# Hybrid diffusion backbone: the last products of the chunk inverse placed between two halves of a recurrence step, and two PSUM users moved to another pool

## The chip, the cores and the metric

One core of one Trainium2 chip runs the whole program. Its engines each work through a queue of their own, in a fixed order: PE (TensorE, matrix products), DVE (VectorE), ACT (ScalarE), POOL (GpSimd), and SP, which here issues the DMAs. The metric is the device time of one execution in microseconds. The kernel before takes 4563.76 us (median of 3 runs, 4554.51 to 4570.26).

## The reference, cut to what matters

Two layers. In each a token mixer and a channel mixer; the change is in the token mixer, which runs two groups of heads side by side over 1024 latent tokens and 256 context tokens: attention (8 heads), and RWKV-7, a linear recurrence in both directions (8 heads of 64). In float32:

```
def step(s, inp):                                   # one token
    r_t, w_t, k_t, v_t, kk_t, a_t = inp
    sa = einsum('bhvk,bhk->bhv', s, kk_t)
    s = (s * w_t[:, :, None, :]
         - sa[..., None] * (kk_t * a_t)[:, :, None, :]
         + v_t[..., None] * k_t[:, :, None, :])
    return s, einsum('bhvk,bhk->bhv', s, r_t)       # state, output
...
for d in range(2):                                  # both directions
    s_ctx, y_c = wkv_scan(..context.., s0, rev=d)
    _, y_l = wkv_scan(..latent.., s_ctx, rev=d)
m_lat = concat([rwkv_output(y_lat[0] + y_lat[1], ..), mla_lat]) @ w_o
```

The two outputs per token (one per direction) are added, normalised per head, gated, put beside the attention's output, and go through one output projection.

## The kernel before, in words

Each layer runs as stages: input projection, mixer, output projection, channel mixer. Only the mixer is touched. It mixes two kinds of work that need nothing of each other.

Attention is cut into pairs of heads `h` and tiles of 128 queries `t`: 40 pieces in layer 0, 32 in layer 1. A piece (`attn`, lines 1037 to 1124) makes scores `sp` on PE (L1075), takes their extreme on DVE (`mx`, L1076), the exponential on ACT (`P`, L1088), transposes it on PE (`tp`, L1107), copies that on DVE or ACT (`pT`, L1112 and L1110), multiplies it with the values on PE (`av`, L1117), and ends with `o` on DVE (L1123).

The recurrence is cut into chunks of 64 tokens: ten steps `i` of 128 tokens, each of two halves `c`, both directions and all heads at once. A step has four parts.

- Preparation, `rwkv_prep`: loads `KR`, `BK`, `W` from DRAM, makes the chunk's products `g` (L884) and transposes `bt` (L894) on PE, masks them on DVE (`KR`, `GA`, L887 and L890) and copies the rest on ACT (`AB`, `BT`).
- Inverse, `rwkv_inv`: `Dg` on ACT (L911), the transpose `Dt` on DVE (L913), then 31 dependent pairs of DVE operations on `T` (L925, L926), and the transposes `TD` (L928) and `X` (L932).
- Last products of the inverse, `rwkv_inv2`: `p1` (L945) needs `TD`; its result goes through ACT and DVE into `AB`; `p2` (L953) needs that; its result goes into `X`. Only the sequence of the same step uses that `X`.
- Sequence, `rwkv_seq(i, c)`: Z (L977, copied at L979), X times Z (L984, to `W` at L985 and L986), the new state (L991, `St` L996, `W` of the next half L999, `S` L1001). Beside that chain the outputs `y` (L1009 and L1014, evicted to `ysb` at L1021 or L1024). L1009 is the last reader of a step's `KR`.

`rwkv_out` normalises and gates `ysb` of the later visits to a block and writes it to DRAM (L838); the output projection (L1187, L1228) reads that.

Two things set the order of the work. The mixer's code order: two preparations ahead, then for each step its share of attention, `rwkv_seq(i, 0)`, `rwkv_seq(i, 1)`, `rwkv_inv2(i + 1)`, `rwkv_prep(i + 2)`. From that the layer underneath fixes an order per engine when the program is built: it takes what is ready in its own reckoning, earlier code first, and waits where a buffer is still held. Buffers of one tag are handed out in code order. PSUM is 8 banks: `Rp` has two for tag "r" (`g`, `bt`, the `ro` of `rwkv_out`), `Rq` one for tag "q" (every product of `rwkv_seq`, and `p1`, `p2`), attention has five. `KR` has two buffers for each direction, so step `i + 2` loads into what step `i` held; `BK` and `AB` have two, `Dg`, `Dt`, `T`, `TD` one.

Of the kernel before, what the change touches and what calls it, by code (L numbers as in the profile page):

```python
# [7 lines left out]
F32 = mybir.dt.float32  # L8
# [14 lines left out]
NP = 4  # L23
# [50 lines left out]
def bc(ap, shape):  # L74
    return ap.to_broadcast(shape)
# [6 lines left out]
class Kern:  # L82
# [675 lines left out]
    def mixer(self, l, wst):  # L758
        tc = self.tc
        with ExitStack() as st:  # L760
            R = self.R = Ctx()
            R.pp = st.enter_context(tc.tile_pool(name=f"Rp{l}", bufs=2, space=PSUM, reuse_waits="tile"))
            R.pq = st.enter_context(tc.tile_pool(name=f"Rq{l}", bufs=1, space=PSUM, reuse_waits="tile"))
            self.attn_setup(l, st)
            self.rwkv_setup(l, st)
            need_ctx = l < DEPTH - 1
            order = ([8, 9] if need_ctx else []) + [3, 4, 2, 5, 1, 6, 0, 7]
            work = [(h, t) for h in range(NP) for t in order]
            done = 0
            self.rwkv_prep(l, 0)  # L770
            self.rwkv_inv2(l, 0)
            self.rwkv_prep(l, 1)
            for i in range(10):

                upto = len(work) * (i + 1) // 10 if i < 9 else len(work)
                for h, t in work[done:upto]:
                    self.attn(l, h, t, t == order[0])
                done = upto
                self.rwkv_seq(l, i, 0)
                self.rwkv_seq(l, i, 1)  # L780
                if i < 9:
                    self.rwkv_inv2(l, i + 1)
                if i == 8:
                    R.sr.close()
                    self.load_wo(l, wst)
                if i < 8:
                    self.rwkv_prep(l, i + 2)
                for o in R.out:
                    self.rwkv_out(*o)
                R.out = []  # L790
# [144 lines left out]
    def rwkv_inv2(self, l, i):  # L935

        nc = self.nc
        R = self.R
        pp, cst = R.pp, self.cst
        AB, TD = R.inv  # L940
        X = R.X[i % 2]
        ps = R.pq.tile([128, 16, 32], F32, name="p1", tag="q")
        for u in range(16):
            for q0 in (0, 64):
                nc.tensor.matmul(ps[q0 + 32:q0 + 64, u, :], AB[q0:q0 + 32, u, 32:64], TD[q0:q0 + 32, u, :],  # L945
                                 start=True, stop=True)
        nc.scalar.activation(AB[96:128, :, 0:32], ps[96:128], AF.Copy, scale=-1.0)
        nc.vector.tensor_scalar(AB[32:64, :, 0:32], ps[32:64], -1.0, None, op0=ALU.mult)
        ps = R.pq.tile([128, 16, 32], F32, name="p2", tag="q")
        for u in range(16):  # L950
            for q0 in (0, 64):
                r = slice(q0 + 32, q0 + 64)
                nc.tensor.matmul(ps[q0:q0 + 32, u, :], AB[r, u, 0:32], X[r, u, 32:64], start=True, stop=True)  # L953
        nc.scalar.activation(X[0:32, :, 32:64], ps[0:32], AF.Copy)
        nc.vector.tensor_copy(X[64:96, :, 32:64], ps[64:96])

    def rwkv_seq(self, l, i, c):

        nc = self.nc
        R = self.R  # L960
        p, pp = R.p, R.pq
        X = R.X[i % 2]
        half = [slice(0, 64), slice(64, 128)]
        tgs = self.groups(i)
        out_y = l < DEPTH - 1 or tgs[0] < 8
        KR, GA, W, BT, PC = R.st.pop((i, c))
        nxt = R.st.get((i + c, 1 - c))
        S = R.S
        dq = [(d, q) for d in range(2) for q in range(NP)]
        psum = lambda: pp.tile([128, 2, NP, 64], F32, name="q", tag="q")  # L970
        if S is None:
            for e in range(2):
                nc.vector.memset(W[half[e], e], 0.0)
        ps = psum()
        for d, q in dq:
            for e in range(2):
                nc.tensor.matmul(ps[half[e], d, q, :], KR[d][:, e, q, c, :], W[:, e, d, q, :], start=True, stop=True)  # L977
        Z = p.tile([128, 2, NP, 64], F32, name="Z", tag="Z")
        nc.vector.tensor_copy(Z, ps)  # L979
        ps = psum()  # L980
        for d, q in dq:
            for e in range(2):
                he = half[e]
                nc.tensor.matmul(ps[he, d, q, :], X[he, (d * 2 + c) * 4 + q, :], Z[he, d, q, :], start=True, stop=True)  # L984
        nc.scalar.activation(W[half[0], 0], ps[half[0]], AF.Copy, scale=-1.0)  # L985
        nc.vector.tensor_scalar(W[half[1], 1], ps[half[1]], -1.0, None, op0=ALU.mult)  # L986
        if nxt is not None:
            ps = psum()
            for d, q in dq:
                for e in range(2):  # L990
                    nc.tensor.matmul(ps[half[e], d, q, :], BT[d][:, q, e, :], W[:, e, d, q, :], start=True, stop=True)  # L991
            St = p.tile([128, 2, NP, 64], F32, name="St", tag="Z")
            if S is None:
                nc.vector.tensor_copy(St, ps)
            else:
                nc.vector.tensor_tensor(St, ps, S, op=ALU.add)  # L996
            pb = bc(PC[:, :, :, None], [128, 2, NP, 64])
            for e, eng in ((0, nc.vector), (1, nc.gpsimd)):
                eng.tensor_tensor(nxt[2][half[e], e], St[half[e]], pb[half[e]], op=ALU.mult)  # L999
            R.S = p.tile([128, 2, NP, 64], F32, name="S", tag="S", bufs=2)  # L1000
            nc.gpsimd.tensor_tensor(R.S, St, pb, op=ALU.mult)  # L1001
        if out_y:
            py = psum()

            if S is not None:
                for d, q in dq:
                    for e in range(2):
                        he = half[e]
                        nc.tensor.matmul(py[he, d, q, :], S[he, d, q, :], KR[d][he, 2, q, c, :], start=(d, q) == dq[0],  # L1009
                                         stop=False, skip_group_check=True)  # L1010
            for d, q in dq:
                for e in range(2):
                    he = half[e]
                    nc.tensor.matmul(py[he, d, q, :], W[:, e, d, q, :], GA[d][:, e, q, :],  # L1014
                                     start=S is None and (d, q) == dq[0], stop=(d, q) == dq[-1], skip_group_check=True)
            ysb = p.tile([128, 2, NP, 64], F32, name="ysb", tag="ysb", bufs=2)
            if self.second(l, i):
                y0 = p.tile([128, 2, NP, 64], F32, name="y0", tag="y0")
                for d, tg in enumerate(tgs):
                    nc.sync.dma_start(out=y0[:, d], in_=self.yD[l][2 * tg + (1 - c if d else c)])  # L1020
                nc.vector.tensor_tensor(ysb, py, y0, op=ALU.add)  # L1021
                R.out.append((l, i, c, ysb))
                return
            nc.scalar.activation(ysb, py, AF.Copy)  # L1024
            for d, tg in enumerate(tgs):
                nc.sync.dma_start(out=self.yD[l][2 * tg + (1 - c if d else c)], in_=ysb[:, d])
# [441 lines left out]
```

## Time and profile before

| | |
|---|---|
| median of 3 runs | 4563.76 us |
| the profiled execution's own time | 4568.71 us |
| its span, first to last instruction | 4566.9 us |
| mixer of layer 0 | about 690 to 1411 us of the span |
| mixer of layer 1 | about 3007 to 3700 us |

The busy time of an engine is the time in which at least one of its instructions ran. The stretches of the two mixers are taken from the first attention work to the last result of the recurrence (L835), and the output projection's first product (L1228) stands after them. A wait is named by what ended it; where a step's result waits for another engine, the row of the waiting instruction names that engine and line.

### The profile page before, as it was taken

Reading aid. Unit: us, or ns where it says so; the run is one execution under the profiler, and the core shown is the slowest. Engines: PE = TensorE matmul, PEld = TensorE weight load, DVE = VectorE, ACT = ScalarE, POOL = GpSimd, SP = SyncE. Lnnn points to the kernel's source line nnn. Section 1 sums busy time; section 2 is a strip of 40 time slices with the busy share of each in tenths; the row PEclk is TensorE's granted clock in tenths of the full one; section 3 lists DMA queues with packets and bytes.
Section 4 is the critical chain, followed back from the end, with each engine's and each line's share of the span. In section 5 each row is a group of like instructions: output and inputs, shape, how many; then the busy total and the mean of one; then the engine's idle time right before and its main releaser. Section 6 shows DMA issues by size and latency. Waiting matters only on the chain. (4 is left out here: it accounts for less than half of the span.)

```text
span 4566.9 us, 72983 instructions
## 1 busy us (share of the span) xinstructions
PE 4159.5 (91%) x29598; PEld 3294.7 (72%) x29598; DVE 2736.5 (60%) x4943; ACT 1688.5 (37%) x3000; POOL 541.9 (12%) x492
## 2 busy tenths in 40 slices
PE   8978888888888899999998989988889878999998
PEld 5756656676766788888886866666777666888887
DVE  3225567888885534554447235569887866555456
ACT  3213455444554432221224224454445534222222
POOL 1000000111222300000004000001111244000002
PEclk9998889899998999999998998989998989999999
DMA  6652234323324211111113222343232243111111
GB/s 222 237 180 91 104 120 125 84 69 81 79 61 140 100 37 35 40 42 33 47 35 111 84 71 100 117 144 77 61 81 66 65 136 126 54 51 51 44 50 65
DMA packets 425698, 401.36 MB, mean 88 GB/s; under 512 B 243473, under 2 KB 329937, under 8 KB 425361
## 3 DMA queue, kind: packets, MB, share of 16 engines
q1 hardware_dynamic: 425360, 396.69, 28.1%
q8 instruction: 233, 3.82, 0.3%
q14 instruction: 105, 0.85, 0.1%
HBM read 285.85 MB, written 110.72 MB: 87 GB/s over the span
## 5 line engine op out<-in xcount | busy, mean ns | idle before, releaser
L1279 PE MATMUL up<-u,hi 128*128 128x512 f32 (+1 forms) x3520 | 1012.6, 369 | 4.2 <-ACT hi L1269 4.2
L1279 PEld LDWEIGHTS up<-u,hi 128*128 128x128 f32 x3520 | 643.8, 189 | 119.8 <-ACT hi L1269 4.6
L1279 PE MATMUL up<-u,lo 128*128 128x512 f32 (+1 forms) x1760 | 648.5, 368 | 0.0
L304 PE MATMUL pj<-u,whi 128*128 128x512 f32 (+1 forms) x1888 | 567.2, 385 | 36.0 <-DVE o L325 31.0
L1326 DVE TENSOR_TENSOR acc<-dn,acc 128x512 f32<-128x512 f32 x340 | 233.3, 688 | 432.9 <-PE dn L1320 432.8
L304 PEld LDWEIGHTS pj<-u,whi 128*128 128x128 f32 x1888 | 352.6, 198 | 139.4 <-issue 45.2
L1279 PEld LDWEIGHTS up<-u,lo 128*128 128x128 f32 x1760 | 332.1, 189 | 57.9 <-DVE lo L1271 0.3
L304 PE MATMUL pj<-u,wlo 128*128 128x512 f32 (+1 forms) x944 | 360.0, 382 | 0.1
L1075 PE MATMUL sp<-ka,qa 96*128 96x512 f32 (+1 forms) x1200 | 320.8, 399 | 37.2 <-ACT P L1088 26.1
L1269 ACT ACTIVATE hi<-raw 128x512 fp32r<-128x512 f32 x176 | 110.5, 630 | 564.4 <-PE up L1279 561.4
L1320 PE MATMUL dn<-hi,fh 128*128 128x512 f32 x792 | 311.8, 394 | 7.9 <-ACT fh L1294 4.0
L1320 PE MATMUL dn<-lo,fh 128*128 128x512 f32 x792 | 310.0, 391 | 0.0
L1320 PE MATMUL dn<-hi,fl 128*128 128x512 f32 x792 | 305.9, 390 | 0.0
L1088 ACT ACTIVATE P<-sp,mx 128x512 f32<-128x512 f32 (+1 forms) x400 | 240.0, 607 | 174.1 <-DVE mx L1085 98.4
L1117 PE MATMUL av<-pT,va 128*64 128x128 f32 x2624 | 235.5, 302 | 51.3 <-DVE pT L1112 25.5
L1075 PEld LDWEIGHTS sp<-ka,qa 96*128 96x128 f32 x1200 | 214.8, 205 | 89.6 <-ACT P L1088 38.5
L1107 PE MATMUL tp<-cst,P 128*128 128x128 f32 x1312 | 236.7, 303 | 22.5 <-ACT P L1088 16.4
L1076 DVE TENSOR_REDUCE mx<-sp 128x1 f32<-128x512 f32 (+1 forms) x400 | 229.4, 586 | 39.7 <-PE sp L1075 37.1
L1117 PEld LDWEIGHTS av<-pT,va 128*64 128x64 f32 x2624 | 152.0, 146 | 108.6 <-DVE pT L1112 31.7
L1271 DVE TENSOR_TENSOR lo<-raw,hi 128x512 fp32r<-128x512 f32 x176 | 125.4, 715 | 173.8 <-ACT hi L1269 161.3
L287 ACT ACTIVATE whi<-raw 128x512 fp32r<-128x512 f32 (+2 forms) x110 | 66.1, 602 | 435.7 <-PE pj L304 384.5
L304 PEld LDWEIGHTS pj<-u,wlo 128*128 128x128 f32 x944 | 186.6, 198 | 39.2 <-issue 7.3
(254 smaller groups left out, 7233.5 us busy)
## 6 DMA issues: line engine op xcount, KB each, us to landing
wt<-in_w_ada_dram SPq DMA_DIRECT2D x96, 512.0 KB
raw<-in_w_up_dram SPq DMA_DIRECT2D x176, 256.0 KB
raw<-in_w_down_dram SPq DMA_DIRECT2D x88, 256.0 KB
raw<-in_w_in_dram SPq DMA_DIRECT2D x84, 256.0 KB
bkD<-lt SPq DMA_DIRECT2D x32, 640.0 KB
BK<-bkD SPq DMA_DIRECT2D x320, 64.0 KB
KR<-kkD SPq DMA_DIRECT2D x152, 128.0 KB
kkD<-kx SPq DMA_DIRECT2D x16, 640.0 KB
```

The lines of the kernel that those rows point to most:

```text
L287: nc.scalar.activation(hi[:, :m], raw[:, :m], AF.Copy)
L304: nc.tensor.matmul(ps[:, o:o + n], ww, u[k][s], start=k == 0 and j == 0, stop=k == nk - 1 and j == 2)
L1075: nc.tensor.matmul(sp[:, o - b0:o - b0 + n], q[:, qq, e], A.k[e][:, kk, o:o + n], start=m == 0, stop=m == 2)
L1076: nc.vector.tensor_reduce(mx[:, i:i + 1], sp[:, :w], axis=AX.X, op=ALU.min)
L1088: nc.scalar.activation(P[:, o:o + w], sp[:, :w], AF.Exp, bias=mn, scale=-1.0, accum_out=mx[:, 4 + i:5 + i])
L1107: nc.tensor.transpose(tp[:, b, e], Ps[e][:, o:o + 128], self.ident)
L1117: nc.tensor.matmul(av[half[e], 0:128], A.v[:, k0 // 128 + kt, half[e]], pT[:, b, e], start=kt == 0, stop=kt == nkt - 1)
L1269: nc.scalar.activation(hi, raw, AF.Copy)
L1271: nc.vector.tensor_tensor(lo, raw, hi, op=ALU.subtract)
L1279: nc.tensor.matmul(ps[:, so:so + sn], ww, uu[k][s], start=k == 0 and m == 0, stop=k == 7 and m == 2)
L1320: nc.tensor.matmul(ps, x[:, t * 128:(t + 1) * 128], w, start=m == 0, stop=m == 3 * len(js) - 1)
L1326: nc.vector.tensor_tensor(dst, ps, dst, op=ALU.add)
```

## The change

Three edits. `rwkv_inv2(i + 1)` now stands between the two halves of step `i` in the code. Its `p1` and `p2` take banks of tag "r" in place of tag "q". The outputs `y` of `rwkv_seq` do so too. No instruction is added or taken away, and no size changes.

```
                 self.rwkv_seq(l, i, 0)
-                self.rwkv_seq(l, i, 1)
                 if i < 9:
                     self.rwkv_inv2(l, i + 1)
+                self.rwkv_seq(l, i, 1)
...
-        ps = R.pq.tile([128, 16, 32], F32, name="p1", tag="q")
+        ps = pp.tile([128, 16, 32], F32, name="p1", tag="r")
...
-        ps = R.pq.tile([128, 16, 32], F32, name="p2", tag="q")
+        ps = pp.tile([128, 16, 32], F32, name="p2", tag="r")
...
         if out_y:
-            py = psum()
+            py = R.pp.tile([128, 2, NP, 64], F32, name="y", tag="r")
```

The order on PE in layer 0 around the outputs of step 7's second half (L1009 and L1014 into `q`), before; `g` in the last row but two is the first of step 9's preparation:

```order
L991 MATMUL q<-W,BT 64x64 x16
L1117 MATMUL av<-pT,va 64x128 x4
L1107 MATMUL tp<-cst,P 128x128 x4
L1075 MATMUL sp<-ka,qa 128x512 x6
L1075 MATMUL sp<-ka,qa 128x256 x3
L1009 MATMUL q<-KR,S 64x64 x16
L1014 MATMUL q<-GA,W 64x64 x16
L1117 MATMUL av<-pT,va 64x128 x4
L1107 MATMUL tp<-cst,P 128x128 x4
L884 MATMUL g<-KR,BK 128x128 x8
L1075 MATMUL sp<-ka,qa 128x512 x3
L1117 MATMUL av<-pT,va 64x128 x4
```

`p1` of step 8 stands 13 rows after that first `g`. The same outputs in the changed kernel (L1009 and L1014 now into `y`), with `p1` and `p2` of step 8 (L945, L953):

```order
L1107 MATMUL tp<-cst,P 128x128 x4
L945 MATMUL p_11935<-TD,AB 32x32 x32
L1117 MATMUL av<-pT,va 64x128 x4
L1120 MATMUL av<-cst,mx 64x128 x2
L1107 MATMUL tp<-cst,P 128x128 x4
L953 MATMUL p_11970<-X_4537,AB 32x32 x32
L1009 MATMUL y<-KR,S 64x64 x16
L1014 MATMUL y<-GA,W 64x64 x16
L984 MATMUL q<-Z,X_4537 64x64 x9
L884 MATMUL g<-KR,BK 128x128 x4
```

The outputs of a step's second half have moved behind `p1` and `p2` of the next step, and the `g` of the step after that stands behind them. It is so at all 16 such places of the two layers that have outputs; at the two in layer 1 that have none (its context steps), `g` stands behind `p2` too.

The order on DVE in layer 0 at the start of step 9's inverse (the last one), before:

```order
L979 COPY Z<-q 128x512
L1076 TENSOR_REDUCE mx<-sp 128x1
L1112 COPY pT<-tp 128x512
L913 STREAM_TRANSPOSE Dt<-Dg 128x1024
L1123 TENSOR_TENSOR o_12607<-av,o_12607 128x128
L1076 TENSOR_REDUCE mx<-sp 128x1
L925 TENSOR_TENSOR tmp<-Dt,T 128x31
L1085 TENSOR_REDUCE mx<-mx 128x1
L926 TENSOR_TENSOR T<-T,tmp 128x31
```

and in the changed kernel:

```order
L986 TENSOR_SCALAR W<-q 64x512
L913 STREAM_TRANSPOSE Dt<-Dg 128x1024
L996 TENSOR_TENSOR St<-q,S 128x512
L925 TENSOR_TENSOR tmp<-Dt,T 128x31
L833 TENSOR_TENSOR ysb<-ysb,sq 128x512
L999 TENSOR_TENSOR W<-St,pc_91 64x512
L926 TENSOR_TENSOR T<-T,tmp 128x31
L1123 TENSOR_TENSOR o_13677<-av,o_13677 128x128
L925 TENSOR_TENSOR tmp<-Dt,T 128x30
```

Before, 180 of layer 0's 208 score reductions (L1076) stand ahead of this `Dt`; in the changed kernel all 208 do, and the `o` in the fence is the last of the 40 pieces of attention. In layer 1 the same holds one step sooner: ahead of `Dt` of step 8 stood 148 of 192 reductions, and now stand all 192. On every engine the output projection begins behind the last instruction of the mixer, in both orders.

## Rows read from the trace of the kernel before

**Rows 1.** The page's head: span and instructions.
```profile
span 4566.9 us, 72983 instructions
```
**Rows 2.** Busy time by stretch: us, then each engine's busy us, PEclk, DMA share, GB/s.
```profile
690.00:1411.00 721.00, 627.74 (x8076) 492.86 (x8074) 582.52 (x1526) 375.05 (x870) 123.57 (x139) 0.93 0.33 84
1080.00:1120.00 40.00, 38.47 (x560) 31.26 (x561) 34.82 (x91) 22.84 (x58) 5.02 (x7) 1.00 0.27 68
1381.00:1411.00 30.00, 21.61 (x244) 15.53 (x240) 13.17 (x23) 17.59 (x30) 7.30 (x6) 0.76 0.36 99
3007.00:3700.00 693.00, 604.29 (x7674) 476.61 (x7673) 560.24 (x1465) 349.89 (x808) 111.50 (x126) 0.91 0.31 81
```
**Rows 3.** PE in order of time, one round: start, us, line, operation; wait in brackets.
```profile
1128.39 1.15 PE L1009 MATMUL q<-KR,S 64*64 64x64 f32 x32
1129.47 1.15 PE L1014 MATMUL q<-GA,W 128*64 128x64 f32 x32
1131.21 0.66 PE L1107 MATMUL tp<-cst,P 128*128 128x128 f32 x4
1133.32 1.99 PE L884 MATMUL g<-KR,BK 64*128 64x128 f32 x16 [1.45 <-DMA KR<-kkD]
...
1175.20 1.15 PE L977 MATMUL q<-W,KR 128*64 128x64 f32 x32 [0.37 <-DVE ysb L1021]
...
1205.28 1.20 PE L945 MATMUL p<-TD,AB 32*32 32x32 f32 x64 [0.28 <-DVE TD L928]
1209.22 1.20 PE L953 MATMUL p<-X,AB 32*32 32x32 f32 x64
```
**Rows 4.** DVE in order of time, the same round.
```profile
1161.88 1.98 DVE L913 STREAM_TRANSPOSE Dt<-Dg 128x1024 f32<-128x1024 f32 x1 [0.43 <-ACT Dg L911]
1168.26 0.68 DVE L999 TENSOR_TENSOR W<-St,pc 64x512 f32<-64x512 f32 x1
...
1204.15 1.07 DVE L928 STREAM_TRANSPOSE TD<-T 128x512 f32<-128x512 f32 x1
```
**Rows 5.** PE in order of time: `p1` of steps 0 and 9, both layers.
```profile
789.27 1.20 PE L945 MATMUL p<-TD,AB 32*32 32x32 f32 x64 [2.04 <-DVE TD L928]
1350.22 1.92 PE L945 MATMUL p<-TD,AB 32*32 32x32 f32 x64
3101.57 1.20 PE L945 MATMUL p<-TD,AB 32*32 32x32 f32 x64
3642.69 1.92 PE L945 MATMUL p<-TD,AB 32*32 32x32 f32 x64
```
**Rows 6.** Groups on DVE, layer 0's mixer: busy us, mean ns of one, idle before.
```profile
L926 DVE TENSOR_TENSOR T<-T,tmp 128x126 f32<-128x126 f32 (+22 forms) x310 | 100.4, 324 | 5.7
L925 DVE TENSOR_TENSOR tmp<-Dt,T 128x126 f32<-128x126 f32 (+22 forms) x310 | 92.4, 298 | 5.2
L887 DVE TENSOR_TENSOR KR<-g,cst 64x256 f32<-64x256 f32 x80 | 33.5, 419 | 21.3 <-PE g L884 20.5
L890 DVE TENSOR_TENSOR GA<-g,cst 128x256 f32<-128x256 f32 x80 | 33.2, 415 | 0.6
```
**Rows 7.** In order of time: the ends of both mixers, and ACT's split of `w_o`.
```profile
1361.01 1.14 ACT L755 ACTIVATE hi<-raw 128x512 fp32r<-128x512 f32 x2
1391.97 1.97 PE L1009 MATMUL q<-KR,S 64*64 64x64 f32 x32 [2.31 <-DVE W L986]
1397.32 1.14 ACT L755 ACTIVATE hi<-raw 128x512 fp32r<-128x512 f32 x2
1408.59 1.26 POOL L835 TENSOR_TENSOR ysb<-ysb,gt 128x512 f32<-128x512 f32 x1 [3.37 <-DMA gt<-gD]
1411.39 0.29 DVE L1123 TENSOR_TENSOR o<-av,o 128x128 f32<-128x128 f32 x1 [4.87 <-ACT o L1122]
1418.74 3.78 PE L1228 MATMUL ps<-hi,mh 128*128 128x512 f32 x8 [7.71 <-ACT mh L1187]
3699.46 1.26 POOL L835 TENSOR_TENSOR ysb<-ysb,gt 128x512 f32<-128x512 f32 x1 [3.66 <-DMA gt<-gD]
```

## The prediction

> **What bounds the kernel now.** I read the page first (its span [rows 1]; the profiled execution took 4568.7 us, 1.8 more than the span and 5 more than the median of the runs), then busy time by stretch, then the two mixers in order of time, engine by engine, and last the groups of DVE. Only the mixers matter, since nothing outside them is edited. In both the reader is to see that two engines are full nearly all the time: in layer 0 PE is busy 627.74 of 721 us (87%) and DVE 582.52 (81%), in layer 1 604.29 and 560.24 of 693 [rows 2]. Attention fills whatever the recurrence leaves. Both end together: the last `o` of attention at 1411.7, the last result of the recurrence at 1409.9, and the output projection's first product at 1418.7 [rows 7].
>
> Under that lies a loop of dependences. After the outputs of a step's second half (PE, 1128.39 to 1130.62) `KR` is free, its DMA lands, and the first `g` of the step after next starts at 1133.32. `Dt` follows at 1161.88, `TD` at 1204.15, `p1` at 1205.28, `p2` at 1209.22 [rows 3, 4]. From the outputs' end to `p1` that is 74.7 us. Steps follow each other faster than that: `p1` of steps 0 and 9 stand at 789.27 and 1350.22, 62.3 us a step, in layer 1 60.1 [rows 5]. That is possible because two such loops run side by side, one for even and one for odd steps: while one step's inverse runs, the next preparation has already begun. So the mixer is bound by the sum of its work at about 87% of PE, and the loop is hidden by its twin.
>
> **The change part by part.** No instruction is added or taken away; three edits change the order and who holds a bank.
>
> The move of `p1` and `p2` ahead of the second half buys no time by itself. They wait for `TD`: `p1` starts 0.06 us after `TD` ends (1204.15 + 1.07) and its wait names `TD`, at step 0 as well, 2.04 us [rows 3 to 5]. At 1205.28 the second half of the step before is over long since. I take 0, and since no row names the bank "q" as what `p1` waits for, neither end is far: a gain of at most those 2 us, a loss only by what follows.
>
> The outputs leave "q". Before, the next half's first product must wait until `ysb` has been taken from that bank: after a first half the next state is in place at 1168.94 (`W`, 1168.26 + 0.68), the next half's Z starts at 1175.20, its wait named `ysb` [rows 3, 4]. That is 6.3 us a step of the sequence's own chain, now free. PE itself idled 0.37 us there, since attention filled it. I take it at 0 where engines are full, and at up to 6.3 us a step below (first rival).
>
> What decides is the third thing, which no row of before shows and the order does: the outputs now share "r" with `p1`, `p2`, `g` and `bt`, banks are given in code order, and `p1`, `p2` of the next step come first. So a second half's outputs stand behind `p2` of the next step on PE, and with them the release of `KR`, its DMAs on SP and the preparation of the step after next. The two loops have become one: outputs, `KR`, preparation, inverse, `p1`, `p2`, outputs. One turn makes one step, where one turn of either loop made two. In before's terms a turn is 74.7 + 7.4 us (`p1` to the end of `p2` 5.1, outputs 2.3) = 82 us [rows 3]. Attention, free of all this, runs ahead and fills the gaps until it is gone. The order says when: in layer 0 at `p1` of step 8, in layer 1 at `Dt` of step 8. What is left then has nothing beside it. So each mixer is a full stretch, as dense as before, and a bare tail.
>
> DMAs move with it: the loads of `KR`, `W` and of the earlier outputs and the stores of `ysb` come later on SP, whose queue also holds attention's loads. A `KR` load that waits longer than reckoned holds those up. I take 0 for that, since attention is ahead of its need, and the `g` rows bound it: the one wait on `KR` there is 1.45 us [rows 3], 26 us if each of 18 steps had it in full and nothing beside it.
>
> *Where the tail begins.* Layer 0, behind `p1` of step 8: on DVE 31 pairs of 0.622 (19.3 us), 16 masks of 0.417 (6.7), and some 52 others, most near the 0.68 of `W` (36), 62 us or 10.6% of 582.5; on PE 20 groups of 1.15 (Z, X, state, outputs; 23), four of 1.2, four rounds of `g` of 1.99 and some 21 others near 0.66 to 1.2 (17), 53 us or 8.4% of 627.7 [rows 2 to 4, 6]. At the old density that is 61 to 76 us of the 721, so `p1` of step 8 would stand at 1411 - 68 = 1343, a spacing of (1343 - 789) / 8 = 69 us. The turn would have to keep that: below the 82 us of before's rows, above a bare turn (7.4 + 2.7 + 22 + 28 = 60, below). I put it 1.5 us a step later: 1355. Layer 1, behind `Dt` of step 8: one inverse more on DVE (62 + 28 = 90 us, 16% of 560) and less attention on PE (45 us, 7.4% of 604), so 51 to 111 us of 693, mean 81; 3700 - 81 + 12 = 3631.
>
> *How long the tail is.* From `p1` of step 8: `p2` and outputs 7.4; `KR` 2.7 (1130.62 to 1133.32); `g` to `Dt` between 15 (four times 1.99 and 16 masks of 0.417, one after the other) and the 28.6 of the row, and I take the middle, 22; `Dt` to `p1` 28 (1.98, 19.3, eight others of 0.68 that the order puts between them, `TD` 1.07) in place of 43.4, the attention between having gone. Then `p1` of step 9 to the end: before 1350.22 to 1409.85 and 3642.69 to 3700.72, 59.6 and 58.0 us; below that stands ACT's split of `w_o`, which starts after `p2` and took 1361.01 to 1398.46 (37.5 us, its loads coming through two buffers), so 5.1 + 37.5 = 43; I take 45. Sum 7.4 + 2.7 + 22 + 28 + 45 = 105 us, and 28 more in layer 1, 133 [rows 3 to 7].
>
> *Sum.* Layer 0 ends at 1355 + 105 = 1460 in place of 1410, layer 1 at 3631 + 133 = 3764 in place of 3701: 50 + 63 = 113 us. 4568.7 + 113 = 4682, less the 5 by which the profiled execution lies above the median: **4677 us**.
>
> PE's clock may add to it. In the last 30 us of layer 0's mixer, with PE busy 21.61 of 30, the granted clock was 0.76, against 1.00 in a stretch with 38.47 of 40, and 32 outputs took 1.97 us in place of 1.15 [rows 2, 3, 7]. At that ratio the tail's PE rows on the chain, some 17 us (`g` 8, `p1` and `p2` 2.4, Z, X and state 4.6, outputs 2.3), would grow by 12. I leave this to the upper end. The Trainium skill (TensorE: Matmul & The Clock Gate, Part 1) says that the low clock is the default and activity releases it; by that rule the whole tail would run low, about 12 us more per layer, and the row at 0.76 agrees in direction.
>
> **The rivals.**
>
> *Faster: the outputs' bank was the brake.* If the full stretch is bound by the sequence's chain, each loop gains the 6.3 us per turn: five turns in layer 0, four in layer 1, 57 us, time 4507. For it: the waits on `ysb` [rows 3]. Against it: attention fills them, and the order shows the tail whatever the stretch does. The Trainium skill (Perfetto Trace Analysis, Optimizing Tensor Performance) has a rule on this side: independent products should rotate through different PSUM banks, so that emptying one overlaps the next. The 6.3 us gap agrees with it; it does not speak of the order in which a pool gives banks out.
>
> *No change: the tail is paid for by a denser stretch.* Attention running ahead always offers PE work. To hide 105 us, `p1` of step 8 must stand at 1305 and the density rise by (1343 - 690) / (1305 - 690) = 6%, PE to 92%; layer 1 needs 10%, to 96%. One stretch of 40 us had 96% [rows 2]. Time 4564. Against it: DVE would have to rise with PE, and the turn would have to fit 64 us.
>
> *Much slower: the turn stays at 82 us.* Then steps come 82 us apart from the start: `p1` of step 8 at 789 + 8 x 82 = 1445, end 1550; layer 1, with `Dt` of step 8 at 3102 + 7 x 82 + 38 = 3714, end 3847; together +286, 4850. For it: every row of before's turn. Against it: before, a turn shared the engines with 1.2 steps of recurrence, now with none but its own, and the attention that it waits behind is gone before the end.
>
> **How the numbers follow.** About 0.3% (14 us) is what a measurement here can tell from no change. The forecast, one loop with a bare tail, 0.75; faster 0.05; paid for 0.06, of which 0.05 within 0.3%; turn at 82 us or most of the way 0.14. The forecast's own range: down by both 12 us, by 14 us of a quicker tail per layer (`g` at 15, `w_o` quicker alone), 4625; and some of the second rival, 4605. Up: half way to the third, (4677 + 4850) / 2 = 4763. Range 4605 to 4765. Slower by over 0.3% holds the forecast, the third and the rest of the second, 0.90; same 0.05; faster 0.05.
>
> **What would show it.** Right: at the end of each mixer a stretch of some 100 us with PE well below half busy and no scores (L1075); outputs of second halves right behind `p2`; the first `g` of the step after next behind them; `p1` spaced 65 to 75 us while attention lasts and 55 to 65 in the tail; the output projection's first product some 50 us later in layer 0, 110 in layer 1. Wrong: `p1` spaced near 62 us as before, or attention still running at the last outputs; a stretch before the tail with PE over 92% (then the second rival); spacing at 82 us (the third).

## The result, and the profile after

The changed kernel takes 4813.72 us (median of 4 runs, 4800.21 to 4834.38) against 4567.01 for the kernel before on the same chip: 5.5% slower, ratio 1.0546 [1.0499, 1.0592], some 247 us. The forecast was 4677 with a range up to 4765. The sign and the kind of loss are as forecast, the size is over twice as large (113 us was forecast). The profiled execution took 4834.38 us, so its rows lie 21 us above the median; those of before lie 5 above theirs.

Nothing outside the mixers changed: layer 0's ends 136 us later than in [rows 7], layer 1's 265 later, and that is the whole difference of the two profiled executions (265.7). Busy time by stretch first, the stretch up to `p1` of step 8 and the rest of each mixer, then one turn after another, cut at `Dt` and `p1` (columns as in [rows 2]):

```profile
690.00:1417.00 727.00, 624.48 (x7013) 492.11 (x7011) 522.62 (x1389) 326.90 (x792) 94.28 (x114) 0.87 0.27 69
1417.00:1545.00 128.00, 68.73 (x1065) 54.30 (x1064) 70.52 (x139) 52.11 (x80) 28.76 (x26) 0.70 0.31 82
3138.00:3832.00 694.00, 578.84 (x6682) 452.79 (x6680) 495.78 (x1332) 303.41 (x738) 80.79 (x99) 0.89 0.25 65
3832.00:3965.00 133.00, 67.55 (x988) 53.77 (x988) 69.59 (x133) 47.91 (x69) 28.75 (x26) 0.62 0.30 78
```
```profile
1013.00:1052.00 39.00, 35.25 (x500) 29.36 (x502) 20.06 (x39) 17.39 (x36) 4.14 (x6) 0.87 0.34 86
1052.00:1096.00 44.00, 36.70 (x278) 27.70 (x273) 35.91 (x109) 15.46 (x44) 5.90 (x8) 0.65 0.19 51
1096.00:1135.00 39.00, 37.07 (x500) 31.09 (x499) 18.42 (x42) 15.75 (x37) 3.25 (x3) 0.86 0.24 61
1135.00:1172.00 37.00, 30.00 (x344) 22.72 (x344) 34.77 (x109) 16.22 (x45) 5.09 (x6) 1.00 0.16 41
```

The reader is to see two things. There is a tail at the end of each mixer, of 128 and 133 us from `p1` of step 8, with PE half busy: that was forecast (105 us from there, PE well below half busy). And the stretch ahead of it is thinner than before: DVE is busy 522.62 of 727 us (72%) where [rows 2] have 81%, in layer 1 71%. The second fence says why. From `p1` to `Dt` (1013 to 1052, 1096 to 1135) DVE is busy for half of the time, PE for more than 90%: `g` is the work. From `Dt` to `p1` (1052 to 1096, 1135 to 1172) DVE is busy for 82 to 94%: the inverse is the work. With one loop these two kinds of stretch alternate; with two they lay side by side. Attention needs both engines, so it finds little room in either kind of stretch.

PE in order of time (start, us, line, operation; wait in brackets), one turn while attention lasts (`p1` of step 3 to `p1` of step 4), as [rows 3] have it of before:

```profile
1012.93 1.20 PE L945 MATMUL p<-TD,AB 32*32 32x32 f32 x64
...
1016.53 1.20 PE L953 MATMUL p<-X,AB 32*32 32x32 f32 x64 [1.23 <-DVE AB L948]
1017.66 1.87 PE L1009 MATMUL y<-KR,S 64*64 64x64 f32 x32
1019.46 1.94 PE L1014 MATMUL y<-GA,W 128*64 128x64 f32 x32
...
1024.00 1.51 PE L884 MATMUL g<-KR,BK 64*128 64x128 f32 x8
...
1096.36 1.20 PE L945 MATMUL p<-TD,AB 32*32 32x32 f32 x64
```

and DVE in the same turn:

```profile
1052.00 1.97 DVE L913 STREAM_TRANSPOSE Dt<-Dg 128x1024 f32<-128x1024 f32 x1
...
1091.17 1.11 DVE L928 STREAM_TRANSPOSE TD<-T 128x512 f32<-128x512 f32 x1
```

This is the loop that the prediction drew: `p1`, `p2`, outputs, `KR`, `g`, `Dt`, `TD`, `p1`. Its pieces are 8.5 us (`p1` to the outputs' end at 1021.40), 2.6, 28.0, 39.2 and 5.2: they have hardly shrunk against [rows 3, 4].

The last turn of layer 0 and what follows it, PE, then DVE in that turn, then POOL's last row of each mixer:

```profile
1417.00 1.20 PE L945 MATMUL p<-TD,AB 32*32 32x32 f32 x64
...
1422.20 1.92 PE L953 MATMUL p<-X,AB 32*32 32x32 f32 x64
1424.05 1.97 PE L1009 MATMUL y<-KR,S 64*64 64x64 f32 x32
1425.95 1.80 PE L1014 MATMUL y<-GA,W 128*64 128x64 f32 x32
...
1429.58 1.13 PE L884 MATMUL g<-KR,BK 64*128 64x128 f32 x8 [1.11 <-DMA KR<-kkD]
...
1486.60 1.92 PE L945 MATMUL p<-TD,AB 32*32 32x32 f32 x64 [19.59 <-DVE TD L928]
```
```profile
1454.55 1.94 DVE L913 STREAM_TRANSPOSE Dt<-Dg 128x1024 f32<-128x1024 f32 x1 [1.61 <-ACT Dg L911]
...
1485.39 1.06 DVE L928 STREAM_TRANSPOSE TD<-T 128x512 f32<-128x512 f32 x1
```
```profile
1544.38 1.26 POOL L835 TENSOR_TENSOR ysb<-ysb,gt 128x512 f32<-128x512 f32 x1 [3.04 <-DMA gt<-gD]
...
3964.35 1.26 POOL L835 TENSOR_TENSOR ysb<-ysb,gt 128x512 f32<-128x512 f32 x1 [2.95 <-DMA gt<-gD]
```

In the tail PE waits 19.59 us for `TD`: attention has run out (its last score ends at 1411.88, its last `o` at 1461.78). And the rows of `p1` that answer to [rows 5], steps 0 and 8 of each layer and step 9 of layer 1 (step 8 of layer 0 and step 9 stand above):

```profile
779.81 1.20 PE L945 MATMUL p<-TD,AB 32*32 32x32 f32 x64
...
3232.40 1.20 PE L945 MATMUL p<-TD,AB 32*32 32x32 f32 x64 [0.77 <-DVE TD L928]
...
3832.43 1.92 PE L945 MATMUL p<-TD,AB 32*32 32x32 f32 x64 [19.39 <-DVE TD L928]
...
3901.75 1.92 PE L945 MATMUL p<-TD,AB 32*32 32x32 f32 x64 [18.78 <-DVE TD L928]
```

From step 0 to step 8 that is (1417.00 - 779.81) / 8 = 79.6 us a step in layer 0 and 75.0 in layer 1, where 69 was forecast.

### The profile page after: what moved, and what is told of

It reads as the page before. It is cut to its first block, busy times and chain, and to the rows that moved or that the text cites. A ratio compares the mean times of both kernels' runs of the same rounds, so it can differ in the third digit from the quotient of the medians.

```text
span 4832.6 us, 73062 instructions
## 1 busy us (share of the span) xinstructions
PE 4261.3 (88%) x29598; PEld 3375.9 (70%) x29598; DVE 2751.8 (57%) x4943; ACT 1694.9 (35%) x3000; POOL 538.0 (11%) x492
## 5 line engine op out<-in xcount | busy, mean ns | idle before, releaser
L1075 PE MATMUL sp<-ka,qa 96*128 96x512 f32 (+1 forms) x1200 | 330.7, 413 | 49.9 <-ACT P L1088 36.8
L1117 PE MATMUL av<-pT,va 128*64 128x128 f32 x2624 | 249.6, 311 | 105.9 <-DVE pT L1112 37.8
L1075 PEld LDWEIGHTS sp<-ka,qa 96*128 96x128 f32 x1200 | 226.9, 215 | 106.3 <-ACT P L1088 52.9
L1076 DVE TENSOR_REDUCE mx<-sp 128x1 f32<-128x512 f32 (+1 forms) x400 | 230.6, 589 | 58.2 <-PE sp L1075 54.9
```

Source lines behind the costliest of these rows:

```text
L1075: nc.tensor.matmul(sp[:, o - b0:o - b0 + n], q[:, qq, e], A.k[e][:, kk, o:o + n], start=m == 0, stop=m == 2)
L1076: nc.vector.tensor_reduce(mx[:, i:i + 1], sp[:, :w], axis=AX.X, op=ALU.min)
L1117: nc.tensor.matmul(av[half[e], 0:128], A.v[:, k0 // 128 + kt, half[e]], pT[:, b, e], start=kt == 0, stop=kt == nkt - 1)
```

## The experiments

The change has three parts, and each was run alone and in pairs: the move of `p1`, `p2` ahead of the second half (M), their banks in "r" (P), the outputs' banks in "r" (Y). The order of a step on PE (Z stands for the second half's first product, y for the last of its outputs, L1014, `g` for the first of the step after next) and the medians, each against the kernel before measured beside it on the same chip:

| kernel | order of most steps on PE | median us | against before |
|---|---|---|---|
| before | Z, y, g, p1, p2 | 4558.70 to 4567.01 | |
| P (e1) | Z, y, p1, p2, g | 4789.01 | +228 |
| Y (e2) | Z, g, y, p1, p2 | 4590.21 | +30 |
| M (e3) | p1, p2, Z, y, g | 4861.97 | +301 |
| P, Y (e4) | Z, y, p1, p2, g | 4798.07 | +238 |
| M, Y (e11) | p1, p2, Z, g, y | 4811.69 | +250 |
| M, P (e12) | Z, y, p1, p2, g | 4796.08 | +237 |
| M, P, Y (after) | Z, p1, p2, y, g | 4813.72 | +247 |

Where y stands behind `g`, the other part of the outputs, L1009, stands ahead of it and has let go of `KR`; in M, Y it stands even ahead of `p1`, and there Z is the last to read a step's `KR`.

Theory A was the prediction's step: the outputs, behind `p2` in "r", hold `KR`. Theory B: with P, `p1` and `p2` themselves stand ahead of the next `g` in "r" and so close the loop, whatever the outputs do. C: one of the parts costs by itself, with no loop.

**e1: P alone** (`p2` likewise).
```diff
-        ps = R.pq.tile([128, 16, 32], F32, name="p1", tag="q")
+        ps = pp.tile([128, 16, 32], F32, name="p1", tag="r")
...
```


> Only p1 and p2 move to the preparation's tag r; the code order and the outputs' bank are as before. Theory A (the prediction's: the loop of the steps is closed because the second half's outputs stand behind p2 of the next step and hold KR): the outputs stay ahead of p1, KR comes free as before, so near before, 4540 to 4600 us, p1 spaced near 62 us in layer 0. Theory B (p1 and p2 take their turn in tag r ahead of the g of the step after next, and that alone closes the loop): most of the loss stays; against the changed kernel a turn lacks only the outputs and the KR load, some 5 us in each of 16 to 18 turns, so 4680 to 4760 us, p1 spaced 70 to 75 us, g directly behind p2. Theory C (two banks are too few for more users of tag r, whatever the order): slower by a part, 4620 to 4720 us.

4789.01 us, ratio 1.0497 [1.0469, 1.0525]. One turn of its PE:

```profile
1050.77 1.15 PE L1009 MATMUL q<-KR,S 64*64 64x64 f32 x32
1051.85 1.15 PE L1014 MATMUL q<-GA,W 128*64 128x64 f32 x32
...
1081.35 1.20 PE L945 MATMUL p<-TD,AB 32*32 32x32 f32 x64 [0.48 <-DVE TD L928]
...
1087.71 1.92 PE L953 MATMUL p<-X,AB 32*32 32x32 f32 x64
1089.56 2.07 PE L884 MATMUL g<-KR,BK 64*128 64x128 f32 x8
```

The outputs end at 1053.00 and `KR` is free; the first `g` starts at 1089.56, as `p2` ends, 37 us later. At all 16 places of the two layers `g` starts within 0.1 us of `p2`'s end. The loop is closed by `p2` to `g`, and no output stands in it. A is out as the main cause. B has the mechanism and, within a microsecond, the spacing (74.1 and 75.6 us from step 0 to step 8), but its range was missed by 29 us.

**e2: Y alone.**
```diff
-            py = psum()
+            py = R.pp.tile([128, 2, NP, 64], F32, name="y", tag="r")
```


> Only the outputs y move to tag r; p1, p2 and the code order are as before. A and B: no p1 stands ahead of anything new, two loops remain, and the next half's first product no longer waits for the outputs' eviction (6.3 us in the row of before): same or faster, 4500 to 4570 us, p1 spaced 58 to 62 us in layer 0. C: a new user of tag r delays g and bt: slower, 4600 to 4700 us.

4590.21 us, ratio 1.0071 [1.0051, 1.0092]: slower by a little, which none of the three had. The recurrence gained (its `p1` of step 9 at 1324 in place of 1350.22) and attention lost: last row of either in layer 0's mixer, POOL and DVE:

```profile
1391.62 1.28 POOL L835 TENSOR_TENSOR ysb<-ysb,gt 128x512 f32<-128x512 f32 x1 [2.32 <-DMA gt<-gD]
...
1444.97 0.29 DVE L1123 TENSOR_TENSOR o<-av,o 128x128 f32<-128x128 f32 x1 [3.28 <-ACT o L1122]
```

Before, both ended within 2 us of each other [rows 7]; here the 17 us that the recurrence won are of no use, since attention ends 53 us behind it. Why it comes late is not settled. Layer 0's mixer as a stretch (columns as in [rows 2]):

```profile
690.00:1446.00 756.00, 665.65 (x8043) 517.32 (x8042) 585.05 (x1526) 369.31 (x863) 124.89 (x139) 0.90 0.32 83
```

PE is as full as before (88%, 87% in [rows 2]), but about as many products took 665.65 us in place of 627.74, at a granted clock of 0.90 in place of 0.93. No run tells the order of the work and the clock apart.

**e3: M alone** (the two lines that call `rwkv_seq(l, i, 1)` and `rwkv_inv2(l, i + 1)` change places, banks as before).

> Only the code order changes (inverse's last products ahead of the second half); all stay in the one bank q. A and B alike: with one bank given in code order the whole second half stands behind p2 of the next step, so a turn holds the second half's chain too (some 15 us more than in the changed kernel, in each of 18 turns): 4950 to 5150 us, p1 spaced 88 to 98 us. C: no new user of tag r, so near before, 4540 to 4600 us.

4861.97 us, ratio 1.0668 [1.0640, 1.0695]: the slowest of all, against C; A and B, alike here, had the direction, with a range (4950 to 5150) and a spacing (88 to 98 us, measured 79.0 and 76.5) that were too high. PE:

```profile
1171.03 1.20 PE L945 MATMUL p<-TD,AB 32*32 32x32 f32 x64
...
1177.24 1.92 PE L953 MATMUL p<-X,AB 32*32 32x32 f32 x64
...
1181.19 1.51 PE L977 MATMUL q<-W,KR 128*64 128x64 f32 x32
...
1194.48 1.15 PE L1009 MATMUL q<-KR,S 64*64 64x64 f32 x32
1195.56 1.15 PE L1014 MATMUL q<-GA,W 128*64 128x64 f32 x32
...
1202.59 1.16 PE L884 MATMUL g<-KR,BK 64*128 64x128 f32 x16
```

The one bank "q" goes to `p1` and `p2` first, so the whole second half, from Z to the outputs, stands behind them and in the turn. So M and P each close the loop by themselves, at another place.

**e4: P and Y.** 

> p1, p2 and the outputs in tag r, but the code order of before. A: the outputs stand ahead of p1 in the code, KR comes free early, so near before, 4520 to 4600 us. B: p1 and p2 still take their turn ahead of the next g, one loop: like p1 and p2 alone in r, 4680 to 4760 us. C: as the changed kernel, near 4810 us, since the same three users share the two banks.

4798.07 us, ratio 1.0527 [1.0498, 1.0556]: A is wrong again. B's range is missed by 38 us and C's figure by 12, so this run does not choose between the two; what C puts it down to, three users of two banks, is put to the test in e6. The order has B's mark: `g` stands right behind `p2` here too.

**e5: P, with the preparation of step i + 2 ahead of `inv2` of step i + 1 in the code**, so that "r" goes to `g` first. **e6: the same with Y.**
```diff
                 self.rwkv_seq(l, i, 0)
                 self.rwkv_seq(l, i, 1)
+                if i < 8:
+                    self.rwkv_prep(l, i + 2)
                 if i < 9:
                     self.rwkv_inv2(l, i + 1)
+                if i < 8:
+                    self.rwkv_inv(l, i + 2, R.AB)
...
-                if i < 8:
-                    self.rwkv_prep(l, i + 2)
...
-        self.rwkv_inv(l, i, AB)
+        R.AB = AB
```


> Edit: p1 and p2 in tag r, outputs in q as before, no move of the second half; but in the code the preparation of step i+2 (without its inverse) now stands ahead of inv2 of step i+1, so that banks of r are given first to g and bt of step i+2 and then to p1, p2 of step i+1. Theory B (what costs is that p1, p2 stand ahead of the next g in r, which makes the two loops one): the two loops are back, first g of a step starts beside the inverse of the step before, p1 spaced 60 to 64 us, time 4540 to 4610, although p1 and p2 still share r. Theory E (sharing r itself is what costs: two banks for g, bt, p1, p2 are too few, whatever the order): time stays at 4700 to 4800 as with p1, p2 in r alone (4789).

> Edit: as e5_p_behind_g, and the outputs in tag r too. Theory B: the two loops are back, time 4540 to 4640 (outputs in r alone cost 30 us because attention fell behind the recurrence; something of that may come with them). Theory E (two banks are too few for all that is put in them, whatever the order): 4700 to 4850. Theory A (my forecast's step: the second half's outputs in r hold KR): no loss here either, since outputs come ahead of p2 in the order.

4630.46 us, ratio 1.0136 [1.0115, 1.0156], and 4613.53, 1.0106 [1.0088, 1.0123]. Of P's loss of 228 us 162 are gone, of P's and Y's 238 us 188, although `p1` and `p2` still share "r": it is the order in which the pool gives its banks, not their number, that makes most of the loss (E is out, and with it C's reading of e4). B's range holds for e6; for e5 it was missed by 20 us, and PE shows the price of the other order (line numbers from L888 on are four higher in this kernel):

```profile
1091.11 1.15 PE L1018 MATMUL q<-GA,W 128*64 128x64 f32 x32
...
1096.06 1.23 PE L888 MATMUL g<-KR,BK 64*128 64x128 f32 x16 [0.21 <-DMA KR<-kkD]
...
1123.39 0.60 PE L898 MATMUL bt<-cst,BK 128*128 128x128 f32 x4
...
1125.10 1.20 PE L949 MATMUL p<-TD,AB 32*32 32x32 f32 x64
```

`TD` of this step was ready at 1103.07; `p1` starts 22 us later, behind the last `bt` of the next preparation. From `p1` of step 0 to that of step 9 steps of layer 0 come 66.8 us apart, not 62.3. Outputs, `g`, `bt`, `p1`, `p2` and the next outputs now stand in one chain, without the inverse in it. Whoever comes first in a shared pool, the other waits; this order only costs less.

**e7, e8: the inverse cut from 31 pairs to 15, in the kernels before and after.**
```diff
-        for j in range(31):
+        for j in range(15):
```


> Kernel before with the elimination in the inverse cut from 31 pairs to 15; it leaves out the last 16 columns of the inverse. Some 16 pairs of 0.62 us or 10 us of DVE a step, 200 us of DVE in all. Theory B (before is set by the sum of work, the turn is hidden): PE, 87% busy, leaves little to gain: 20 to 100 us faster, 4460 to 4540. Rival D (before and after are set alike, after only with less overlap): as much as in the next kernel.

> Kernel after with the elimination in the inverse cut from 31 pairs to 15; it leaves out the last 16 columns of the inverse. Theory B (after, one turn of the loop makes one step, so each microsecond in the turn is paid 18 to 20 times): 10 us of DVE, with the attention that slips between them up to 14, off each turn: 180 to 280 us faster, 4530 to 4630. Rival D (sum of work with less overlap): falls as the kernel before does, 20 to 100 us, 4710 to 4790.

Before: 4575.57 us, ratio 1.0028 [1.0006, 1.0050]: a shorter inverse brings nothing at all (B's 20 to 100 was too much). Layer 0's mixer in that kernel, up to its end:

```profile
690.00:1463.00 773.00, 682.40 (x8080) 533.91 (x8079) 515.99 (x1209) 375.91 (x873) 123.26 (x139) 0.87 0.32 84
```

DVE fell from 582.52 to 515.99 us and PE stayed full (88%). Yet this mixer ends at 1462, 51 us later than before, with attention last: PE took 682.40 us for what were 627.74, at a granted clock of 0.87 in place of 0.93. In layer 1, at 0.93 in place of 0.91, the mixer is 13 us shorter than before from its first scores to its last result. So in this execution the zero hides a loss in one layer, at a lower clock, and a gain in the other; why the clock was lower, no run tells.

After: 4604.85 us, 209 less than the changed kernel in full, ratio to before 1.0093 [1.0065, 1.0122]. Steps 0 to 8 of layer 0 come 62.8 us apart in place of 79.6, in layer 1 60.8 in place of 75.0; `p1` of steps 0 and 8 in layer 0:

```profile
759.29 1.92 PE L945 MATMUL p<-TD,AB 32*32 32x32 f32 x64
...
1261.79 1.20 PE L945 MATMUL p<-TD,AB 32*32 32x32 f32 x64 [1.16 <-DVE TD L928]
```

One cut is worth nothing where the inverse is hidden and 209 us where it stands in the loop: the changed kernel is set by the length of the turn, and D is out. With the short turn, attention ends last again, and PE is busy for 89% of layer 0's mixer.

**e9: Y alone, with attention earlier.** Since attention came late in e2, its share ahead of each step was made a tenth larger.
```diff
-                upto = len(work) * (i + 1) // 10 if i < 9 else len(work)
+                upto = len(work) * (i + 2) // 10 if i < 9 else len(work)
```


> Edit: the outputs alone in tag r, as in e2_y_only (4590, slower by 0.7% because attention ended 53 us behind the recurrence in layer 0), and the share of attention that the code puts ahead of each step a tenth larger ((i + 2) of 10 in place of (i + 1)), so that attention comes earlier in the order of work. Theory B: the two loops stay, attention and recurrence end together again, 4540 to 4575, no slower than before. Rival (outputs in r cost by themselves, by two banks for more users): 4580 to 4600, as e2.

4575.68 us, ratio 1.0034 [1.0017, 1.0051]. That is just above B's range and below the rival's. Half of e2's loss is gone, and the rest is at the edge of what can be told. In the profiled execution, the slowest of the 12, the two ends lie 9 us apart (1432.7 and 1441.8), later than before's. Of all versions none beats the kernel before.

**e10: `w_o` loaded and split behind step 9 in place of step 8**, in the kernel after (`if i == 8:` becomes `if i == 9:`). It asks why `p1` of step 9 to the last result took 59 and 64 us and not 45.

> Kernel after with the loads and splits of w_o placed behind step 9 in the code in place of step 8. Theory T (in the tail, ACT's queue holds w_o's splits ahead of the recurrence's own ACT work, which is why p1 of step 9 to the last result took 58 and 63 us and not the 45 that I forecast): that stretch falls to 40 to 50 us; the output projection then waits for w_o, so that the time as a whole stays or grows by up to 60 us (4800 to 4875). Rival (the low granted clock and the chain's own length set it): 55 to 63 us as now.

```profile
1472.50 1.91 PE L945 MATMUL p<-TD,AB 32*32 32x32 f32 x64 [19.82 <-DVE TD L928]
...
1530.15 1.26 POOL L835 TENSOR_TENSOR ysb<-ysb,gt 128x512 f32<-128x512 f32 x1 [3.01 <-DMA gt<-gD]
```

58.9 us (61.3 in layer 1): as in the changed kernel, and at 4820.34 us the whole stands where it stood. But the edit did not move what it was to move. ACT's first split of `w_o`, in the changed kernel and then in e10:

```profile
1492.57 1.13 ACT L755 ACTIVATE hi<-raw 128x512 fp32r<-128x512 f32 x2
```
```profile
1478.47 1.13 ACT L755 ACTIVATE hi<-raw 128x512 fp32r<-128x512 f32 x2
```

In both it starts 6.0 us after `p1` of step 9, and the splits lie among the recurrence's own work on ACT in nearly the same order. So e10 is no test of theory T, which stays open. That ACT's queue holds the chain is seen in the changed kernel's own tail: X times Z ends at 1523.33, ACT begins to copy its half to `W` at 1529.18, after two splits and two operations of `rwkv_out` (L830, L831), and PE waits for that:

```profile
1529.81 0.47 PE L1014 MATMUL y<-GA,W 128*64 128x64 f32 x2 [6.48 <-ACT W L985]
```

**e11: M and Y. e12: M and P**, which undoes in the kernel after just the step that the forecast took for the cause.

> Kernel after with p1 and p2 put back in bank q (the move and the outputs in r stay). Theory B: p1, p2 of the next step come ahead of the second half's first product in q, so that this half, its outputs and with them the KR of the step after next wait for TD: one loop, as in e3_move_only (4862), 4780 to 4880. Rival C (the move costs nothing by itself, as I forecast, and only r matters): 4560 to 4620.

> Kernel after with the outputs alone put back in bank q (the move, and p1, p2 in r, stay). This undoes the one step that my forecast held for the cause. Theory A (the outputs behind p2 in r hold KR): the loops come apart again, 4560 to 4680. Theory B (p1, p2 stand ahead of the next g in r, outputs or not): as after, 4780 to 4840.

4811.69 us, ratio 1.0568 [1.0537, 1.0599], and 4796.08, 1.0510 [1.0448, 1.0573]. B in both. The loop in the changed kernel is closed twice: put `p1`, `p2` back and the move holds the second half behind them; put the outputs back and P still holds `g`, which in e12 starts as `p2` ends at all 16 places, as in e1.

## Why the prediction was wrong in size

*What bounds before: right.* Two loops side by side and the sum of the work, PE's above all: e7 takes 67 us or 11% of DVE's work out of layer 0's mixer and PE is busy for 88% of it, as before (87%); the time as a whole stays.

*The move at 0: wrong by itself, of no account in the sum.* Alone it costs 301 us (e3). With P it costs 9 (237 against 228, e12 and e1), less than the two intervals can tell.

*What makes one loop of the two: wrong step, right result.* "The outputs now share r with p1, p2, g and bt ... and with them the release of KR": the sentence names all the users of "r" and then follows only the outputs. `p1` and `p2` alone do it, by standing ahead of `g` (e1, e12); the outputs add some 10 us at most (238 against 228, e4 and e1; 247 against 237, after and e12), which is again less than the intervals can tell. Layer 1's first steps, which have no outputs, say so in the changed kernel's own trace: `p1` of steps 0 and 1 stand 72 us apart (47 before).

*How long the dense stretch is: the step that failed.* I worked out the spacing, 69 us, from "the old density", and let the turn fit in ("the turn would have to keep that"). It is the other way round: the turn sets the spacing, and the density follows. The rows of before gave the turn as 82; measured 79.6 and 75.0. I argued it down because a turn now shares the engines with less recurrence. But attention stayed, and slips between the pairs of the inverse as before: `Dt` to `TD` takes 40.2 us in the mean of steps 2 to 8 in layer 0, 45.7 before, against 30.8 in the bare turn. e8 shows that the turn is what is paid. In layer 0 this moved `p1` of step 8 from 1355 to 1417, 62 us (71.5 of spacing, less the 9.5 by which `p1` of step 0 came sooner than before); in layer 1, counted from `p1` of step 0, by 43 (600 in place of 557).

*How long the tail is: all terms but one too small.* From the rows above, forecast in brackets: `p1` to the outputs' end 10.8 (7.4), `KR` 1.8 (2.7), `g` to `Dt` 25.0 (22), `Dt` to `p1` 32.1 (28), sum 69.6 (60); `p1` of step 9 to the end 59.0 (45). 128.6 us in place of 105, 133.2 in layer 1. For the last and largest I had [rows 5, 7]: 59.6 and 58.0, and took it down to 45 because `w_o`'s split seemed the floor. No row spoke for less, and the row stood; what fills the 59 us, ACT's queue, the clock or the chain's own length, stays open (e10). PE's clock, left to the upper end, is part of the rest: granted 0.70 and 0.62 in the two tails, so not low throughout, as the prediction had reckoned for the worst, and `p2`, the outputs and `p1` of step 9 took 1.8 to 1.97 us in place of 1.15 to 1.2.

The sum closes: 62 + 24 in layer 0 and 43 + 28 in layer 1, less 5 by which layer 1's `p1` of step 0 lost less than layer 0's end, are 152 us, and 4834 - 4682 is 152.

*The rivals.* The third, the turn at 82 us from the start, stood at 4850 with a chance of 0.14: it was nearly the truth, 36 us above the median, and every row of before spoke for it. That it came so near is in part luck: in layer 0 its `p1` of step 8 stood 28 us late (1445) and its tail of 105 was 24 short. The first is refuted: without its wait the recurrence does gain, 17 us in layer 0 (e2) where the rival had five turns of 6.3, 31 us, and then attention ends last. The Trainium skill (Perfetto Trace Analysis, Optimizing Tensor Performance) advises rotating independent products through different PSUM banks; e2, which moves the outputs to other banks and changes nothing else, took 30 us more and not less, so for that order the measurement decides against it. In the other order the same move took 17 us off (e6 against e5), little more than the intervals can tell. The second is refuted as well: the stretch grew thinner, not denser.

*The signs.* No scores in the tail, outputs behind `p2` and `g` behind them came as forecast. The tail's spacing was 69.6 and 69.3 us (55 to 65 forecast), and PE was busy for 54% and 51% of the tails, not well below half.

## What to carry to other kernels

When a tile moves into a pool that rotates, list everyone else in that pool and ask who now stands ahead of whom: two independent chains that shared a pool's turns became one chain here, in either order, and the order set the price (228 us or 66). Then compute the length of that loop from the rows as they are, and let it set the spacing; an average density is a result of how the chains overlap and can't be carried over to another overlap. And where a row has a duration for the same piece of work, an argument for less needs a row of its own. After an experiment, look in its trace whether the edit moved what it was to move: e10's did not.

## What the runs showed of the hardware that was not expected

With the inverse halved, the kernel before lost none of its time, and PE's granted clock in layer 0's mixer was 0.87 in place of 0.93, with PE's busy time up from 627.74 to 682.40 us for about as many products. In the changed kernel too they took longer: 693.21 us in layer 0's mixer, where PE idles more, and 646.39 in layer 1's, against 627.74 and 604.29 before. In the tails, where PE stood idle nearly half of the time and for up to 19.59 us at once, the granted clock was 0.62 to 0.70, between the two levels of 1.2 and 2.4 GHz (0.5 and 1.0 of full speed), so that part of each tail ran at the lower. No run here held the clock fixed, so how much of the tail, or of the 247 us, it cost stays open.
